# Every fifth full segment of softmax weights transposed by TensorE from fp32, and the filler spread anew

## The chip, the core and the metric

The kernel runs on one core of one Trainium2 chip. The metric is the device time of one execution in microseconds (us), as the median of the runs shown; lower is better. The profile is one execution of its own, taken by the hardware profiler.

## The reference

One decoder block in fp32 on a sequence of 4096 rows of width 1024, with 16 learned rows set before it (4112 positions). After an RMS norm one projection gives the inputs of two groups of heads: eight forgetting-attention heads (FoX) and eight RWKV-7 heads, all of width 64. Their outputs go through one output projection, the residual is added, and a final RMS norm follows.

```python
def _fox_block(q, k, v, cq, ck, q_start):          # 128 queries, all keys up to them
    s = jnp.einsum('bhqd,bhkd->bhqk', q, k).astype(jnp.float32) / math.sqrt(HEAD_DIM)
    s = s + cq[..., :, None] - ck[..., None, :]     # c: cumulated log of the forget gate
    s = jnp.where(k_pos[None, :] <= q_pos[:, None], s, NEG_INF)
    p = jax.nn.softmax(s, axis=-1)
    return jnp.einsum('bhqk,bhkd->bhqd', p, v.astype(jnp.float32))

def _rwkv7_step(S, inp):                            # a scan over 4112 positions
    r_t, w_t, k_t, v_t, a_t, b_t = inp
    sa = jnp.einsum('bhij,bhj->bhi', S, a_t)
    S = S * w_t[:, :, None, :] + sa[..., None] * b_t[:, :, None, :] + v_t[..., None] * k_t[:, :, None, :]
    return S, jnp.einsum('bhij,bhj->bhi', S, r_t)
```

## The kernel before

Precision is kept with pairs of fp16 numbers: a value is split into a high part and a remainder, and a product is made of two or three fp16 matmuls.

**Recurrence.** The rows of RWKV-7 are taken in sub-blocks of 128 positions (`subs`, 33 of them) with four chunks of 32 each; one chunk is three steps (hops) of a chain, each some small matmuls, a copy from PSUM on ScalarE and VectorE, and the next matmuls (`rwkv_chain`, matmuls psz, psu, pso). Beside each hop stand pieces of the work that prepares the sub-block after next and finishes the last one (`rwkv_pre`, `rwkv_pre2`, `rwkv_post`). `rwkv_post` ends with a normalization of the output (lines 874 to 884), TensorE transposes (psd, line 887) and a store (line 894); for the last sub-block it is called once more behind the loop, without a priority.

**Filler.** The projections of the input (`in_proj`: ps_in; queries and keys `qk_block`: ps_qk; values and gate `vz_block`: ps_vz; the other gate `gate_block`: ps_zr) are a generator, `fill`, which is drawn from in units of 48 matmuls of 256 columns: beside the recurrence each hop adds RATE = 0.33 units to a credit and draws until it is spent (line 941). What is left is drawn in attention, together with the output projection of the RWKV half (`rwkv_out`: matmuls ps_p, 24 for a tile of 128 rows, counted as 0.5 units): after each tile of attention until the share of the filler drawn, `spent`, has reached the share of the attention work done (line 1211). Where attention needs projections that aren't made yet, `projected` (line 981) draws them uncounted.

**Attention.** Heads are taken one after the other, each in 32 tiles of 128 queries. A tile's keys, 144 to 4112 of them, are cut into segments of 1024 (SEG). Score matmuls (ps_q, two PSUM buffers of 1024 columns) are evicted by VectorE (line 1051), which adds the gate's bias and keeps the running maximum; ScalarE makes the exponential in place (`sp`, fp32, line 1065) and copies it to fp16 (`hl`, line 1071); GpSimd for 60% of the segments (POOL_SHARE), else VectorE, makes the remainder (line 1076); a DMA transpose on the SP queue turns both halves at once (`ht<-hl`, 128x2048 fp16 for a full segment, line 1078); then TensorE multiplies `ht` with V (ps_o). `attention` is a generator in three parts: scores; exponential to transpose; weights times V. `advance` runs the first part of tile i, then the third of tile i-1 (`finish`), then the second of tile i. There are 9 buffers of `sp` (NSP) and 6 each of `hl` and `ht` (NHL).

**Last head.** In the eighth head the output rows of the attention half are made beside the tiles: load, TensorE transpose (ps_t, line 1233), output projection (ps_p), residual, final norm, store (`out_prep`, `out_rows`).

**Order.** The order on each engine is fixed when the program is built: a scheduler ranks instructions by their priority (an offset for attention of 100000, for filler in attention of 97000, for the chain of 300000) and by a model of when operands are ready. On the chip each engine takes its instructions in that order and waits where an operand is late. All matmuls go through `mm` (line 92); most instructions beside the recurrence are recorded under line 67.

## Time and profile before

| what | value |
|---|---|
| median of 3 runs | 4477.23 us (4459.99 to 4483.77) |
| the profiled execution | 4462.28 us, its span 4460.4 us |
| granted TensorE clock, mean over the span | 0.916 of full speed |
| TensorE (PE) busy | 3912.1 us, 88% of the span |
| VectorE (DVE) busy | 2956.9 us, 66% |
| GpSimd (POOL) busy | 2230.5 us, 50% |
| ScalarE (ACT) busy | 2122.7 us, 48% |
| DMA | 755.37 MB, mean 169 GB/s |

Busy time is the union of the instructions of an engine; matmuls overlap one another, so a burst of them counts from the first start to the last end. PEld is the weight load, beside PE. PEclk is the share of the TensorE clock that was granted, between two levels: 1.00 (2.4 GHz) and 0.50 (1.2 GHz). The DMA share is the mean busy share of the core's 16 DMA engines; packets of two queues can be under way in one engine at a time, so it can pass 1. A wait is put down to what ended it.

The kernel has stretches with different work: preparation (to about 401 us), the recurrence (to 1984), attention (first scores at 2122, last tile done at 4361), and the last output rows.

### The profile page before, as it was taken

Reading aid. Unit: us, or ns where it says so; the run is one execution under the profiler, and the core shown is the slowest. Engines: PE = TensorE matmul, PEld = TensorE weight load, DVE = VectorE, ACT = ScalarE, POOL = GpSimd, SP = SyncE. Lnnn points to the kernel's source line nnn. Section 1 sums busy time; section 2 is a strip of 40 time slices with the busy share of each in tenths; the row PEclk is TensorE's granted clock in tenths of the full one; section 3 lists DMA queues with packets and bytes.
Section 4 is the critical chain, followed back from the end, with each engine's and each line's share of the span. In section 5 each row is a group of like instructions: output and inputs, shape, how many; then the busy total and the mean of one; then the engine's idle time right before and its main releaser. Section 6 shows DMA issues by size and latency. Waiting matters only on the chain. (4 is left out here: it accounts for less than half of the span.)

```text
span 4460.4 us, 106426 instructions
## 1 busy us (share of the span) xinstructions
PE 3912.1 (88%) x42336; PEld 3012.8 (68%) x42336; DVE 2956.9 (66%) x6217; ACT 2122.7 (48%) x4338; POOL 2230.5 (50%) x3289
## 2 busy tenths in 40 slices
PE   5689999999989899998878878888888878978888
PEld 4577777777767677777656655666666656666566
DVE  5346665666667666752878978677787758646774
ACT  5433333333333233321666757577676747524552
POOL 4137565667666665762445545444454435332340
PEclk8899999999876899899999989999999989989989
DMA  9963223323222344324999999999999999999995
GB/s 265 262 172 93 79 79 97 87 75 90 74 70 79 85 138 121 98 88 141 196 213 229 216 193 227 199 216 227 208 212 234 212 203 223 258 270 242 198 218 185
DMA packets 1702644, 755.37 MB, mean 169 GB/s; under 512 B 1444601, under 2 KB 1639601, under 8 KB 1692162
## 3 DMA queue, kind: packets, MB, share of 16 engines
q1 hardware_dynamic: 1489346, 502.84, 55.8%
q10 hardware_dynamic: 194624, 170.08, 15.3%
q0 software_dynamic: 18176, 75.66, 5.6%
q8 instruction: 332, 5.44, 0.5%
q14 instruction: 166, 1.36, 0.1%
HBM read 278.97 MB, written 158.50 MB: 98 GB/s over the span
## 5 line engine op out<-in xcount | busy, mean ns | idle before, releaser
L1076 POOL TENSOR_TENSOR hl<-sp,hl 128x1024 f16<-128x1024 f32 (+7 forms) x384 | 719.7, 1881 | 517.3 <-ACT hl L1071 440.7
L1065 ACT ACTIVATE sp<-sp,nm 128x1024 f32<-128x1024 f32 (+8 forms) x672 | 644.5, 962 | 223.5 <-DVE nm L1057 175.6
L1071 ACT ACTIVATE hl<-sp 128x1024 f16<-128x1024 f32 (+8 forms) x672 | 568.2, 872 | 366.1 <-DMA ht<-hl 239.4
L92 PE MATMUL ps_o<-Vt,ht 128*128 128x64 f16 (+3 forms) x8960 | 559.5, 211 | 180.6 <-DMA ht<-hl 177.8
L92 PE MATMUL ps_q<-K,Q 128*128 128x512 f16 (+4 forms) x2432 | 596.9, 366 | 119.4 <-DVE mt L1051 118.3
L758 POOL TENSOR_TENSOR tm<-X,Am 128x248 f32<-128x248 f32 (+30 forms) x1023 | 498.1, 487 | 376.6 <-DMA Am<-a_d 290.1
L92 PEld LDWEIGHTS <-ht 128*128 128x128 f16 (+1 forms) x8960 | 466.9, 100 | 315.0 <-DMA ht<-hl 204.9
L92 PEld LDWEIGHTS <-wu 128*128 128x128 f16 (+1 forms) x5476 | 513.1, 102 | 194.8 <-ACT wu L160 28.1
L760 POOL TENSOR_TENSOR X<-X,tm 128x248 f32<-128x248 f32 (+30 forms) x1023 | 517.7, 506 | 76.6
L67 PEld LDWEIGHTS <-wu 128*128 128x128 f16 (+1 forms) x4988 | 454.5, 101 | 114.3 <-issue 26.0
L1051 DVE CUSTOM_DVE_ANT_0 sp<-ps_q,cb,mt 128x1024 f32<-128x1024 f32 (+8 forms) x416 | 436.1, 1048 | 80.3 <-PE ps_q L92 40.8
L1076 DVE TENSOR_TENSOR hl<-sp,hl 128x1024 f16<-128x1024 f32 (+8 forms) x288 | 383.2, 1333 | 99.3 <-ACT hl L1071 98.1
L92 PEld LDWEIGHTS <-Q 128*128 128x128 f16 x2432 | 221.8, 100 | 294.8 <-issue 150.2
L67 PE MATMUL ps_in<-fu,wu 128*128 128x256 f16 x3108 | 416.0, 285 | 3.4 <-DVE car L67 3.4
L1051 DVE CUSTOM_DVE_ANT_0 sp<-ps_q,cb,scs 128x1024 f32<-128x1024 f32 (+7 forms) x256 | 297.6, 1164 | 71.2 <-POOL hl L1076 43.9
L92 PE MATMUL ps_qk<-fu,wu 128*128 128x256 f16 x1632 | 237.7, 280 | 24.0 <-DVE t1k L500 18.5
L92 PE MATMUL ps_vz<-wu,fu 128*128 128x256 f16 x1644 | 247.6, 284 | 1.0 <-ACT th L544 0.6
L92 PE MATMUL ps_p<-OH,yH 128*128 128x512 f32 x512 | 221.5, 433 | 29.0 <-DVE oxt L1144 27.5
L1070 POOL MEMSET hl<- 128x224 f16 x256 | 72.4, 287 | 336.8 <-DMA ht<-hl 318.4
L92 PE MATMUL ps_zr<-fu,wu 128*128 128x256 f16 x1536 | 224.8, 285 | 8.0 <-DVE nm L1057 6.3
L67 PE MATMUL psz<-UV,SC 32*64 32x64 f32 (+1 forms) x4128 | 222.4, 232 | 3.0 <-ACT UV L67 2.2
L92 PE MATMUL ps_p<-OH,yL 128*128 128x512 f32 x512 | 209.6, 411 | 0.0
(350 smaller groups left out, 6976.6 us busy)
## 6 DMA issues: line engine op xcount, KB each, us to landing
fu<-u_d POOLq DMA_DIRECT2D x32, 1024.0 KB, 6.8
fu<-u_d SPq DMA_DIRECT2D x30, 1024.0 KB
pr<-p_d SPq DMA_DIRECT2D x32, 832.0 KB
p_d<-prt SPq DMA_DIRECT2D x96, 256.0 KB
u_d<-u SPq DMA_DIRECT2D x16, 1024.0 KB
Am<-a_d SPq DMA_DIRECT2D x128, 128.0 KB
Q<-qk_d ACTq DMA_DIRECT2D x128, 128.0 KB
oxt<-in_x_dram ACTq DMA_DIRECT2D x32, 512.0 KB
```

The costliest lines, as they stand in the source:

```text
L67: r = f(*args, **kw)
L92: PE.matmul(o, lhsT=l, rhs=r, start=start, stop=stop)
L758: G.tensor_tensor(out=tm[:, :, :k], in0=bc(X[:, :, s:s + 1], [P, 8, k]), in1=bc(Am[:, s * C + s + 1:s * C + C].unsqueeze(1), [P, 8, k]), o ...
L760: G.tensor_tensor(out=X[:, :, s + 1:], in0=X[:, :, s + 1:], in1=tm[:, :, :k], op=ALU.add)
L1051: V.tensor_tensor_reduce(out=sp[:, a - a0:b - a0], in0=ps[:, :b - a], in1=head[c][2][:, a - o:b - o], scale=scs[:, p, 0, hp:hp + 1], scala ...
L1065: A.activation(sp[:, :n], sp[:, :n], AF.Exp, bias=nm[:, 0:1], accum_out=nm[:, 1 + a // SEG:2 + a // SEG])
L1070: G.memset(hl3[:, :, n:], 0.0)
L1071: A.activation(hl3[:, 0, :n], sp[:, :n], AF.Copy)
L1076: eng.tensor_tensor(out=hl3[:, 1, :n], in0=sp[:, :n], in1=hl3[:, 0, :n], op=ALU.subtract)
```

## The change

One in five full segments (PE_SHARE = 20) of the exponentials isn't split and turned by DMA: TensorE transposes `sp` itself, in fp32, eight times 128x128, into a PSUM tile that takes its place among the score buffers (tag `q`); ScalarE copies it to fp16 as the high half of `ht`, and VectorE makes the low half from the PSUM tile and that copy. The buffers become 5 of `hl`, 8 of `sp` and 8 of `ht` (NHT); GpSimd makes the remainder of 75% of the segments that go by DMA. A tile's third part may run up to LAG = 2 tiles later, as long as the segments of the waiting tiles and the new one fit the 8 buffers of `ht`. RATE falls to 0.265. What `projected` draws is counted as `spent`, and a tile of `rwkv_out` counts 1.0. In the last head the output rows follow the tiles that are finished.

```diff
--- before.py
+++ after.py
@@ -38,15 +38,17 @@
 NREST = 26
 SEG = 1024
 CH = 1024
-NHL, NSP = 6, 9
+NHL, NSP, NHT = 5, 8, 8
+PE_SHARE = 20
 HEADS = (4, 5, 0, 1, 2, 3, 6, 7)
-POOL_SHARE = 60
+POOL_SHARE = 75
 FILL = 1.0
 PASS_OF = (2, 2, 1, 3)
 QM = 12
 PSTEP = 2
-RATE = 0.33
+RATE = 0.265
 LEAD = 6
+LAG = 2
 PARTS = ((0, 0), (0, 1), (1, 0))
 P_SHIFT = 15 * math.log(2.0)
 
@@ -980,8 +982,9 @@
 
         def projected(p, t):
 
+            nonlocal spent
             while done[PASS_OF[p]] * NB < min(t, SEQ + 1):
-                next(late)
+                spent += next(late)
 
         def head_load(h, c):
 
@@ -1008,12 +1011,13 @@
             c = min(x // CH, NCH - 1)
             return c, x - c * CH
 
-        nseg = 0
+        nseg, npe = 0, 0
+        spent = 0
         qz = {}
 
         def attention(h, i, head, dst):
 
-            nonlocal nseg
+            nonlocal nseg, npe
             p, hp = divmod(h, 2)
             q0 = 64 * hp
             if i % 4 == 0:
@@ -1064,6 +1068,18 @@
                 sp = sps[a // SEG]
                 A.activation(sp[:, :n], sp[:, :n], AF.Exp, bias=nm[:, 0:1], accum_out=nm[:, 1 + a // SEG:2 + a // SEG])
                 nt = -(-n // P)
+                ht = at.tile([P, 2 * SEG // P, P], F16, tag="ht", name="ht", bufs=NHT)[:, :2 * nt]
+                hts.append(ht)
+                if n == SEG:
+                    npe += PE_SHARE
+                    if npe >= 100:
+                        npe -= 100
+                        pt = ps_q.tile([P, nt, P], F32, tag="q", name="ps_w")
+                        for j in range(nt):
+                            PE.transpose(pt[:, j], sp[:, j * P:(j + 1) * P], ident)
+                        A.activation(ht[:, :nt], pt, AF.Copy)
+                        V.tensor_tensor(out=ht[:, nt:], in0=pt, in1=ht[:, :nt], op=ALU.subtract)
+                        continue
                 hl = at.tile([P, 2 * SEG], F16, tag="hl", name="hl", bufs=NHL)[:, :2 * nt * P]
                 hl3 = hl.rearrange("p (a k) -> p a k", a=2)
                 if n % P:
@@ -1074,9 +1090,7 @@
                     nseg += 1
                     eng = G if nseg * POOL_SHARE % 100 < POOL_SHARE else V
                 eng.tensor_tensor(out=hl3[:, 1, :n], in0=sp[:, :n], in1=hl3[:, 0, :n], op=ALU.subtract)
-                ht = at.tile([P, 2 * SEG // P, P], F16, tag="ht", name="ht", bufs=NHL)[:, :2 * nt]
                 SP.dma_start_transpose(out=ht, in_=hl)
-                hts.append(ht)
             yield
             pso = ps_o.tile([P, P], F32, tag="o", name="ps_o")
             for a, ht in zip(range(0, W, SEG), hts):
@@ -1167,39 +1181,40 @@
                 op = os_.enter_context(tc.tile_pool(name="op", bufs=2, side="left"))
                 OW = out_weights(ow, 4)
                 for _ in rwkv_out(op, OW):
-                    yield 0.5
-
-
-        left = sum(max(0, NFULL - done[i]) * n for i, n in ((1, 2), (2, 4), (3, 4))) + 0.5 * NT
+                    yield 1.0
+
+
+        left = sum(max(0, NFULL - done[i]) * n for i, n in ((1, 2), (2, 4), (3, 4))) + NT
         late = filler()
         total = left / FILL
-        work, spent = 0, 0
-        before = None
+        work = 0
+        waiting = []
+
+        segs = lambda i: -(-(N_META + P * (i + 1)) // SEG)
 
         def finish():
-            nonlocal before
-            if before is not None:
-                h, i, gen, yo = before
-                next(gen)
-                if HEADS.index(h) == 7:
-                    DQ.dma_start(yf_d[i * P:(i + 1) * P, h * HD:h * HD + HD], yo[:, i % 4])
-                elif i % 4 == 3:
-                    DQ.dma_start(yf_d[(i - 3) * P:(i + 1) * P, h * HD:(h + 1) * HD]
-                                 .rearrange("(s t) e -> t s e", t=P), yo)
-            before = None
+
+            h, i, gen, yo = waiting.pop(0)
+            next(gen)
+            if HEADS.index(h) == 7:
+                DQ.dma_start(yf_d[i * P:(i + 1) * P, h * HD:h * HD + HD], yo[:, i % 4])
+            elif i % 4 == 3:
+                DQ.dma_start(yf_d[(i - 3) * P:(i + 1) * P, h * HD:(h + 1) * HD]
+                             .rearrange("(s t) e -> t s e", t=P), yo)
 
         def advance(hx, i):
 
-            nonlocal before, yo
+            nonlocal yo
             h = HEADS[hx]
             fetch(hx, i)
             if i % 4 == 0:
                 yo = at.tile([P, 4, HD], F32, tag="yo", name="yo")
             gen = attention(h, i, heads[h], yo[:, i % 4])
             next(gen)
-            finish()
+            while waiting and (len(waiting) > LAG or sum(segs(w[1]) for w in waiting) + segs(i) > NHT):
+                finish()
             next(gen)
-            before = h, i, gen, yo
+            waiting.append((h, i, gen, yo))
 
         yo = None
         for hx in range(7):
@@ -1243,19 +1258,26 @@
             V.scalar_tensor_tensor(out=xt, in0=xt, scalar=ss[:, 1:2], in1=fnw, op0=ALU.mult, op1=ALU.mult)
             DQ.dma_start(out[i * P:(i + 1) * P], xt)
 
-        ready = None
+        ready, row = None, 0
+
+        def rows(n):
+
+            nonlocal ready, row
+            while row < n:
+                nxt = out_prep(row)
+                if ready is not None:
+                    out_rows(row - 1, *ready)
+                ready = nxt
+                row += 1
+
         for i in range(NT):
             with tc.high_priority(offset=PR[4]):
                 advance(7, i)
-            if i > 0:
-                nxt = out_prep(i - 1)
-                if ready is not None:
-                    out_rows(i - 2, *ready)
-                ready = nxt
-        finish()
-        nxt = out_prep(NT - 1)
-        out_rows(NT - 2, *ready)
-        out_rows(NT - 1, *nxt)
+            rows(waiting[0][1] if HEADS[7] == waiting[0][0] else 0)
+        while waiting:
+            finish()
+        rows(NT)
+        out_rows(NT - 1, *ready)
 
 
 _INS = ['x', 'meta', 'norm_w', 'w_in', 'b_f', 'mu_shift', 'w0', 'w_up', 'a0', 'a_up', 'k_k', 'k_a', 'r_k',
```

The line numbers of the changed kernel are 2 to 15 higher. Three places show how the order moves.

On VectorE, between the normalization of the last recurrence output and the first use of attention's loads. `Yt` (line 892, after: 894) finishes that output, `identb` (line 975, after: 977) is the first write into the buffers of attention, `cb` the bias of the first head; `qk`, `vt` and `t1k` are evictions of filler. Before:

```order
L67 SCALAR_TENSOR_TENSOR t1k<-t1k 128x256
L67 TENSOR_TENSOR t1k<-t1k,fnb 128x256
L67 SCALAR_TENSOR_TENSOR qk<-ps_qk,sqs,qk 128x256
L67 SCALAR_TENSOR_TENSOR qk<-ps_qk,qk 128x256
L494 SCALAR_TENSOR_TENSOR vt<-ps_vz,vt 128x2x64 x2
L500 TENSOR_TENSOR t1k<-ps_vz,fnb 128x256
L892 TENSOR_TENSOR Yt<-Yt,bon 128x128
L975 CAST identb<-ident 128x128
L503 SCALAR_TENSOR_TENSOR t1k<-t1k 128x256
L505 TENSOR_TENSOR t1k<-t1k,fnb 128x256
L998 TENSOR_SCALAR cb<-cb,scs 128x1024 x3
```

After, from the normalization's last step (line 886) on:

```order
L886 TENSOR_TENSOR Y<-Y,gva 32x512
L505 SCALAR_TENSOR_TENSOR t1k<-t1k 128x256
L183 TENSOR_SCALAR ss<-pss 128x1
L507 TENSOR_TENSOR t1k<-t1k,fnb 128x256
L894 TENSOR_TENSOR Yt<-Yt,bon 128x128
L977 CAST identb<-ident 128x128
L195 SCALAR_TENSOR_TENSOR wst<-wst,psb 128x1024
L199 COPY fnb<-psb 128x128
L462 TENSOR_SCALAR fnb<-fnb 128x128
L1001 TENSOR_SCALAR cb<-cb,scs 128x1024 x3
```

Before, 52 rows of filler's evictions stand between that step (line 884) and the row of `Yt`; now there are 3. On TensorE 912 filler matmuls stand before the transposes of this output, and now 48.

On VectorE in attention, the scores of tile 30 (counted from 0, four segments) of the fourth head (line 1051, after: 1055, is the eviction of scores; `mt` its maximum; `nm` the maximum or the sums of a tile). Before:

```order
L1051 ISA sp,mt<-ps_q,cb,scs 128x1024
L1051 ISA mt 128x1
L545 SCALAR_TENSOR_TENSOR zt_40139<-th_40140,zt_40139 128x512
L1076 TENSOR_TENSOR hl<-sp,hl 128x1024
L1051 ISA sp,mt<-ps_q,cb,mt,scs 128x1024
L1051 ISA mt 128x1
L1051 ISA sp,mt<-ps_q,cb,mt,scs 128x1024
L1051 ISA mt 128x1
L1096 TENSOR_REDUCE nm<-nm 128x1
L1100 TENSOR_TENSOR o_41699<-ps_o,o_41699 128x64
L1097 RECIPROCAL nm<-nm 128x1
```

After, from the tile's second segment on; line 1081 makes the low half from the TensorE transposes in PSUM:

```order
L1055 ISA sp,mt<-ps_q,cb,mt,scs 128x1024
L1055 ISA mt 128x1
L1081 TENSOR_TENSOR ht<-ps_w,ht 128x1024
L1114 TENSOR_TENSOR o_42277<-ps_o,o_42277 128x64
L1115 SCALAR_TENSOR_TENSOR yo<-o_42277,nm,Zt 128x64
L1055 ISA sp,mt<-ps_q,cb,mt,scs 128x1024
L1055 ISA mt 128x1
L1055 ISA sp,mt<-ps_q,cb,mt,scs 128x912
L1055 ISA mt 128x1
L1061 TENSOR_SCALAR nm<-mt 128x1
```

Before, a filler eviction, a remainder (line 1076, SBUF to SBUF) and the end of an earlier tile stood between the score evictions. Now the row of line 1081, for a segment of an earlier tile, stands there; the score matmul that takes its PSUM buffer is issued behind it.

On the SP queue, tiles of the first head with one, two and three segments (the middle number is twice the segment's columns over 128). Before:

```order
L1078 DMA_TRANSPOSE ht<-hl 128x12x128
L1078 DMA_TRANSPOSE ht<-hl 128x16x128
L1078 DMA_TRANSPOSE ht<-hl 128x14x128
L1078 DMA_TRANSPOSE ht<-hl 128x16x128 x4
L1078 DMA_TRANSPOSE ht<-hl 128x2x128
L1078 DMA_TRANSPOSE ht<-hl 128x16x128 x2
L1078 DMA_TRANSPOSE ht<-hl 128x4x128
L1078 DMA_TRANSPOSE ht<-hl 128x16x128 x2
```

After:

```order
L1093 DMA_TRANSPOSE ht<-hl 128x12x128
L1093 DMA_TRANSPOSE ht<-hl 128x16x128
L1093 DMA_TRANSPOSE ht<-hl 128x14x128
L1093 DMA_TRANSPOSE ht<-hl 128x16x128 x3
L1093 DMA_TRANSPOSE ht<-hl 128x2x128
L1093 DMA_TRANSPOSE ht<-hl 128x16x128 x2
L1093 DMA_TRANSPOSE ht<-hl 128x4x128
L1093 DMA_TRANSPOSE ht<-hl 128x16x128
L1093 DMA_TRANSPOSE ht<-hl 128x6x128
L1093 DMA_TRANSPOSE ht<-hl 128x16x128 x2
```

The rows stand in the same sequence; where a full segment goes to TensorE its row is missing.

## Rows read from the trace of the kernel before

**Rows 1.** Five stretches: time, busy time (instructions) by engine, PEclk, DMA share, GB/s.
```profile
core 0: us, PE busy (x) PEld busy (x) DVE busy (x) ACT busy (x) POOL busy (x), PEclk, DMA share, GB/s
401.00:1984.00 1583.00, 1524.57 (x19786) 1197.15 (x19784) 1022.50 (x2242) 520.02 (x1302) 1033.12 (x2025) 0.91 0.32 89
1984.00:2085.00 101.00, 100.69 (x924) 90.07 (x923) 28.98 (x80) 18.25 (x47) 31.23 (x45) 1.00 0.30 109
2085.00:2122.00 37.00, 18.50 (x153) 15.58 (x151) 6.99 (x15) 1.55 (x4) 6.21 (x15) 0.72 0.83 223
2122.00:4361.00 2239.00, 1884.84 (x18027) 1397.21 (x18025) 1649.51 (x3403) 1391.23 (x2660) 996.61 (x907) 0.93 1.12 220
4361.00:4460.00 99.00, 86.43 (x392) 68.20 (x390) 49.75 (x74) 24.62 (x44) 8.11 (x15) 0.97 0.50 184
```

**Rows 2.** TensorE's timeline: start, length (us), instructions that follow one another.
```profile
1982.55 0.66 PE L67 MATMUL psd<-ident,Y 128*128 128x128 f32 x4
1983.28 5.41 PE L67 MATMUL ps_vz<-wu,fu 128*128 128x256 f16 x48
1988.53 1.69 PE L67 MATMUL ps_qk<-fu,wu 128*128 128x256 f16 x14
```

**Rows 3.** VectorE's timeline behind the recurrence.
```profile
1994.18 0.68 DVE L884 TENSOR_TENSOR Y<-Y,gva 32x512 f32<-32x512 f32 x1 [1.56 <-POOL gva L882]
2084.63 0.29 DVE L892 TENSOR_TENSOR Yt<-Yt,bon 128x128 f32<-128x128 f32 x1 [0.26 <-ACT Yt L891]
2098.56 0.76 DVE L998 TENSOR_SCALAR cb<-cb,scs 128x1024 f32<-128x1024 f32 x1 [12.71 <-DMA cb<-c_d]
```

**Rows 4.** TensorE's waits in attention: us in all, times, longest.
```profile
PE ps_o L92 <- DMA ht<-hl: 177.8, 87, 11.0
PE ps_q L92 <- DVE mt L1051: 118.3, 104, 7.1
```

**Rows 5.** SP queue: timeline of attention; its issues (ns min/median/max).
```profile
2125.56 2224.22 SPq L1078 DMA_TRANSPOSE ht<-hl  x672
...
L1078 SPq DMA_TRANSPOSE ht<-hl x672: 1167/2134/12831, 2125.6 to 4347.2; - x168
```

**Rows 6.** DMA queues of the page: packets, MB, share of 16 engines.
```profile
q1 hardware_dynamic: 1489346, 502.84, 55.8%
q0 software_dynamic: 18176, 75.66, 5.6%
```

**Rows 7.** The four quarters (8 tiles each) of the second head.
```profile
2384.00:2413.00 29.00, 25.28 (x251) 18.42 (x249) 23.25 (x64) 21.29 (x50) 12.84 (x18) 0.96 1.03 221
2413.00:2458.00 45.00, 40.94 (x445) 30.04 (x442) 43.91 (x95) 34.79 (x69) 24.05 (x22) 1.00 1.10 215
2458.00:2520.00 62.00, 54.53 (x582) 41.33 (x581) 54.92 (x103) 45.53 (x84) 34.45 (x28) 0.94 1.11 220
2520.00:2636.00 116.00, 86.58 (x928) 63.21 (x927) 85.26 (x167) 65.02 (x120) 54.65 (x54) 0.87 1.22 209
```

**Rows 8.** Groups by shape: xcount, busy us, mean ns, idle before, releasers.
```profile
L1071 ACT ACTIVATE hl<-sp 128x1024 f16<-128x1024 f32 x416 | 430.0, 1050 | 193.9 <-DMA ht<-hl 126.1 <-issue 17.5 <-PE ps_q L92 9.8
L1076 POOL TENSOR_TENSOR hl<-sp,hl 128x1024 f16<-128x1024 f32 x240 | 532.6, 2223 | 412.3 <-ACT hl L1071 338.6 <-issue 29.8 <-DMA fnw<-in_final_norm_w_dram 19.6
L1076 DVE TENSOR_TENSOR hl<-sp,hl 128x1024 f16<-128x1024 f32 x176 | 271.5, 1543 | 53.3 <-ACT hl L1071 52.4 <-DMA Zt<-zf_d 0.6
L1051 DVE CUSTOM_DVE_ANT_0 sp<-ps_q,cb,scs 128x1024 f32<-128x1024 f32 x200 | 255.3, 1276 | 56.9 <-POOL hl L1076 33.3 <-PE ps_q L92 20.8 <-PE ps_o L92 0.7
```

**Rows 9.** The output rows' TensorE transposes, line 1233: ns min/median/max.
```profile
L1233 PEld LDWEIGHTS ps_t<-ident,yf x128: 137/140/231, 4090.1 to 4440.6; 128*128 128x128 f32 x128
L1233 PE MATMUL ps_t<-ident,yf x128: 269/273/476, 4090.1 to 4440.7; 128*128 128x128 f32 x128
```

**Rows 10.** Two sub-blocks of the recurrence: one without filler, one with.
```profile
1382.00:1435.00 53.00, 50.63 (x529) 38.67 (x527) 40.45 (x89) 14.27 (x37) 31.77 (x63) 0.50 0.30 81
1645.00:1695.00 50.00, 50.00 (x666) 39.55 (x664) 32.37 (x69) 16.68 (x43) 32.35 (x67) 1.00 0.43 118
```

## The prediction

> **What bounds the kernel now.** I read the profile first as five stretches: the recurrence, a gap behind it, the wait for the first attention loads, attention, and the tail after the last attention tile [rows 1]. In the recurrence TensorE is busy 1524.6 of 1583 us, so it idles 58 us or 3.7%: this stretch is as long as TensorE's work, chain and filler together. The 101 us behind it (1984 to 2085) hold nothing but filler: 924 matmuls, busy 100.7 us, one every 0.109 us (48 matmuls from 1983.28 to 1988.53) [rows 1, 2]. VectorE's timeline shows why that hurts: the last step of the recurrence's output (line 884) is done at 1994.2, the step behind it (line 892) comes at 2084.6, because its TensorE transpose stands behind the filler; the first attention loads, which take over its buffers, are used only at 2098.6 [rows 3]. So here filler holds up attention.
>
> In attention (2122 to 4361) TensorE is busy 1884.8 of 2239 us: 354 us idle, 15.8% [rows 1]. Half of this is one wait: the weights-times-V matmuls wait for the DMA transposes, 177.8 us in 87 waits; the score matmuls wait for a free score buffer, which VectorE empties, 118.3 us [rows 4]. The DMA engines stand behind the first: their share is 1.12 over the stretch [rows 1], the SP queue issues its 672 transposes from 2125.6 on over 2224 us, one per 3.3 us, while single issues took from 1.2 to 12.8 us, 2.1 in the median [rows 5]. In the quarters of one head the idle share of TensorE is 13%, 9%, 12% and 25%, and the DMA share is highest, 1.22, in the last [rows 7]. So attention is bound by TensorE and the transposes together, the last quarter of each head by the transposes.
>
> **The change part by part**, against the profiled execution: 4462.3 us, of which 4460.4 are its span. The median of the runs shown, 4477.2, is 15 us higher, and I add that at the end.
>
> Less filler beside the recurrence. By the built order 6096 filler matmuls stand between the chain's first and last matmul now, 5760 after: 336 fewer at 0.109 us is 37 us. Between the chain's last matmul and the first score matmul stand 1074 now and 201 after: 873 fewer, 95 us. The wait for the first loads, 37 us, stays. What this uncovers: the chain's own latency, which is covered by 58 us of idle time only, so I take both terms whole and keep 0 for the first as the other end (see the rivals).
>
> Attention gets the filler: 1209 matmuls more, 132 us of TensorE time.
>
> The TensorE transposes: one in five full segments is 83 segments, 664 transposes of 128x128 in fp32. Four such transposes of the recurrence take 0.66 us from the start of the first to the end of the last, with 0.27 us for one alone, so one follows the other in 0.13 us [rows 2, 9]; the weight load of one takes 0.14 us [rows 9]. At 0.14 us this is 93 us; with each standing alone at 0.273 us it would be 181 us, which I keep for the range, and nothing here lets them cost less than 0.13, 86 us. I take 93, as they are issued by eights.
> By the Trainium skill (TensorE: Matmul & The Clock Gate, Part 4: PE-mode transpose) a 128x128 bf16 transpose costs some 275 ns in a kernel. By that the 664 would be an estimated 183 us, 90 us more, and the forecast some 4500 us. The rows' 0.14 us decides, since they are fp32 transposes of this kernel, issued one behind the other.
>
> The DMA transposes that go: 83 of 128x2048 fp16, 0.524 MB each, 43.5 MB. The SP queue's packets took 55.8% of the 16 engines' span for 502.8 MB, 4.95 us per MB [rows 6], so 215 us of engine time go. The moved filler, 25 units of 48 matmuls, brings about 13.5 MB (a 1 MB block of activations for four units, and their outputs) on GpSimd's queue at 3.3 us per MB [rows 6]: 45 us. DMA time in attention goes from 1.12 x 2239 = 2508 to 2338 us: a share of 1.00 over the length forecast below.
>
> The other engines. ScalarE makes 83 copies from PSUM instead of 83 from SBUF, 1.05 us each [rows 8]: nothing, since it is busy 1391 of 2239 us. VectorE's subtractions go from 288 to 172 and 83 from PSUM, between the 1.28 us of a score eviction, which reads PSUM too, and 1.54 us [rows 8]: some 50 us less on an engine that is 74% busy, so no gain counted. GpSimd's go from 384 to 417, 33 x 2.22 = 73 us on an engine busy 997 of 2239 us: hidden; if its cover is gone, 33 x 0.68 = 22 us for the slower engine. One buffer fewer for the fp16 pairs and for the scores stands against a fifth fewer users: counted at nothing.
>
> The tail. After the last weights-times-V matmul stand 336 output matmuls now and 144 after. The tail's 392 matmuls take 86.4 us [rows 1], 0.22 us each; 192 of them, 42 us, move into attention.
>
> The idle time is the large unknown. TensorE's work in attention becomes 1885 + 132 + 93 + 42 = 2152 us. Its idle share now is 15.8%; the recurrence, dense with filler and with a DMA share of 0.32, has 3.7%. These are my ends. I take 8%, near the 9% that a second quarter of a head has now [rows 7]: the DMA share falls, two more buffers for transposed weights and the longer lag give a transpose a tile more of time, and there is 24% more filler to stand between the waits (4950 matmuls now, 6159 after). Attention is then 2152 / 0.92 = 2339 us, 100 us longer.
> Sum: -37 - 95 + 100 - 42 = -74 us; 4388, and on the scale of the medians 4403 us.
> From it follows the point of decision: the medians' 4477 is met at 261 us of idle time in attention (10.8%), and each us of idle time is a us of the result.
>
> **The rivals.**
> 1. The score buffers take over from the DMA wait. The transposes write to the two PSUM buffers of the scores. One of the 83 holds its buffer for the ScalarE copy and the VectorE subtraction, 1.05 + 1.54 us, and by the new order the next score stands behind it on VectorE. For: score matmuls wait 118 us already, and ScalarE and VectorE work in order. Against: VectorE is 74% busy, filler can stand in between. If 1 us of each 2.6 is filled, 83 x 1.6 = 133 us come in while the wait for transposes falls to a third, -118: idle time 369 us, and the time is 4403 + 182 = 4585 us. It decides from 261 us of idle time on.
> 2. The recurrence doesn't get shorter. A sub-block without filler had a granted clock of 0.50 and took 53 us, one full of filler at 1.00 took 50 us [rows 10]: what the filler gives back, the clock takes. Against: four fifths of the filler stays. Then the 37 us are lost: 4440 us; the 95 us of the gap, where no chain runs, stay.
> 3. The transposes pull the clock down in attention. It is at 0.93 over the stretch [rows 1] and at 0.87 in the last quarter of a head [rows 7]; of the two levels, 1.2 and 2.4 GHz, the lower then holds for 14% and for 26% of the time. If all of attention fell to 0.87, 12% of 2339 us more would run at half speed: 281 us, of which 92% busy, and half of that is lost, 129 us: 4532 us. Against it: of the 128 transposes of the output rows the median is 273 ns and the longest 476 [rows 9], so most ran at the higher level.
> The same Part 4 of the Trainium skill says that transposes don't count as TensorE activity for the clock; what rows show of it is that median alone, and here they stand between other matmuls.
> 4. The new order keeps everything busy as in the recurrence, 3.7% idle: 2235 us of attention, 4299 us.
>
> **How the numbers follow.** Forecast 0.50, rival 1 0.24, rival 2 0.12, rival 3 0.08, rival 4 0.06. Range: it leaves out the far end of rival 1 and the end of rival 4: 4320 (4.6% idle) to 4550 us (13.4% idle); the forecast's own range, 6% to 10.5% idle, is 4353 to 4469. About 0.5%, 22 us, is what a measurement of this kernel can tell from no change, so faster needs under 239 us idle, slower over 283. Faster: most of the forecast (0.41), most of rival 2 (0.09), rival 4 (0.06): 0.56. Slower: rival 1 and rival 3 mostly, and a little of the forecast: 0.28. The rest, 0.16, is no change.
>
> **What would show it.** Between the recurrence's last step and the first score about 95 us fewer; the recurrence some 37 us shorter, at a clock of 0.90 or more. In attention 664 transposes about 0.14 us apart, a DMA share near 1.0, the wait for transposes under 90 us and that for score buffers not over 150. A tail near 57 us. The forecast is wrong if attention takes over 2413 us: then either the score buffers' wait has grown (rival 1), the clock is lower (rival 3), or the wait for DMA stayed near 178 us although the share fell.

## The result and the profile after

The changed kernel takes 4630.07 us (median of 4 runs, 4621.53 to 4669.09) against 4478.23 us before (4 runs, 4459.99 to 4483.77): 1.036 times as long, 95% interval 1.030 to 1.043. The forecast was 4403 us, faster; its range ended at 4550. The profiled execution of the changed kernel is its longest, 4669.1 us, so the two profiles differ by 207 us where the medians differ by 152.

The stretches after, which answer to [rows 1] (time, busy time of each engine, granted clock, DMA share); the pure filler behind the recurrence is gone as a stretch of its own:

```profile
core 0: us, PE busy (x) PEld busy (x) DVE busy (x) ACT busy (x) POOL busy (x), PEclk, DMA share, GB/s
401.00:1967.00 1566.00, 1482.25 (x19490) 1162.56 (x19487) 1022.06 (x2226) 519.33 (x1292) 1019.83 (x2009) 0.91 0.31 88
1967.00:2002.00 35.00, 21.86 (x155) 17.42 (x155) 9.88 (x20) 3.46 (x9) 7.35 (x15) 0.75 0.81 213
2002.00:4621.00 2619.00, 2178.02 (x20127) 1655.85 (x20125) 1719.63 (x3500) 1423.50 (x2735) 1091.82 (x1006) 0.91 0.87 181
4621.00:4667.00 46.00, 36.54 (x170) 29.06 (x167) 22.02 (x33) 10.73 (x20) 3.85 (x7) 0.96 0.46 167
```

Attention begins 120 us earlier (2002 for 2122) and the tail is 53 us shorter, but attention itself takes 2619 us for 2239. TensorE works 293 us more in it, and idles 2619 - 2178 = 441 us, 16.8%, where the forecast had 8%. The DMA engines, which the forecast saw behind that idle time, are less loaded than it hoped: a share of 0.87, some 2280 us of their time for the 2338 forecast. Yet the wait for them grew. TensorE's waits after, against [rows 4], and two waits that name the cause, on VectorE and ScalarE:

```profile
PE ps_o L94 <- DMA ht<-hl: 266.6, 115, 12.3
PE ps_q L94 <- DVE mt L1055: 53.0, 43, 10.8
PE ps_w L1079 <- ACT sp L1069: 24.6, 14, 4.4
DVE sp L1055 <- PE ps_q L94: 326.4, 237, 10.8
ACT sp L1069 <- DVE nm L1061: 383.2, 128, 12.4
```

The same two waits in the kernel before (us in all, times, longest), and the largest wait of the SP queue's transposes for their input, before and after:

```profile
DVE sp L1051 <- PE ps_q L92: 64.7, 55, 4.3
ACT sp L1065 <- DVE nm L1057: 175.6, 91, 14.5
SPq L1078 <- POOL hl L1076: 256.8, 135, 7.4
SPq L1093 <- POOL hl L1092: 731.5, 172, 15.6
```

Read them as a chain. VectorE now waits 326 us for score matmuls, 65 before: the scores come late, and no longer for want of a free buffer (53 us for 118). ScalarE then waits 383 us for the maximum that closes a tile's scores, 176 before. So the exponential, the fp16 pair and the transpose all start late, and the weights-times-V matmuls wait for the transpose although its queue has room: the queue itself waits 732 us for GpSimd's remainders, 257 before. GpSimd makes a larger share of them now, but in e3, below, with its share of before, the queue waits 440 us for GpSimd's and 468 for VectorE's (96 before).

Why the scores are late is in the timeline of TensorE at the end of the fourth head (start, length, instructions in a row, in brackets the idle time ahead of them):

```profile
3217.64 1.03 PE L94 MATMUL ps_q<-K,Q 128*128 128x512 f16 x4
...
3219.70 0.17 PE L94 MATMUL ps_q<-dmask,identb 128*128 128x16 bf16 x1
...
3225.72 3.72 PE L94 MATMUL ps_vz<-wu,fu 128*128 128x256 f16 x21 [3.65 <-ACT th L546]
3236.12 3.04 PE L94 MATMUL ps_o<-Vt,ht 128*128 128x128 f16 x32 [6.68 <-DMA ht<-hl]
3238.97 0.46 PE L1079 MATMUL ps_w<-ident,sp 128*128 128x128 f32 x1
3239.22 0.45 PE L94 MATMUL ps_q<-K,Q 128*128 128x144 f16 x2
```

of VectorE, the eviction of tile 31's last scores:

```profile
3228.88 0.28 DVE L1055 CUSTOM_DVE_ANT_0 sp<-ps_q,cb,mt 128x16 f32<-128x16 f32 x1
```

and of ScalarE, the first and the last exponential of the same tile:

```profile
3229.58 1.15 ACT L1069 ACTIVATE sp<-sp,nm 128x1024 f32<-128x1024 f32 x1 [3.91 <-DVE nm L1061]
...
3234.12 0.29 ACT L1069 ACTIVATE sp<-sp,nm 128x16 f32<-128x16 f32 x1
```

The last scores of tile 31 are done at 3219.9. The next scores (144 keys, tile 0 of the next head) start at 3239.2, behind the first TensorE transpose of tile 31's exponentials. The pool hands out its two buffers in the order in which the program asks for them, and the program asks for the transposes' buffer between the scores of one tile and those of the next. So the next scores can't be issued before this tile's exponential is there, 19 us in which TensorE has filler, idles 3.65 and 6.68 us, and has no score to do. Not all of the 19 us is the exponential, which ends at 3234.4: VectorE evicts the last scores only 9 us after they are done, behind other work, and the 32 products that stand ahead of the transposes on TensorE (tile 30's) wait for their own DMA until 3236.1. The built order shows the same loss of distance: behind the last score of tile 29 of the fourth head stands the weights-times-V product of tile 26 in the kernel before, and that of tile 28 in the changed one. The scores ran three tiles ahead of the products, and now run one. Counted so in the traces, over tiles 20 to 31 of all heads, the scores' lead is 3.2 tiles on average before and 1.3 after.

The steps that came as forecast: VectorE behind the recurrence, against [rows 3]:

```profile
1965.74 0.67 DVE L886 TENSOR_TENSOR Y<-Y,gva 32x512 f32<-32x512 f32 x1
1968.49 0.29 DVE L894 TENSOR_TENSOR Yt<-Yt,bon 128x128 f32<-128x128 f32 x1 [1.08 <-ACT Yt L893]
1980.51 0.75 DVE L1001 TENSOR_SCALAR cb<-cb,scs 128x1024 f32<-128x1024 f32 x1 [1.97 <-DMA cb<-c_d]
```

Here 2.8 us lie between the two steps that were 90 us apart. And the transposes themselves (ns min/median/max), beside [rows 8, 9]:

```profile
L1079 PEld LDWEIGHTS ps_w<-ident,sp x664: 137/141/231, 2044.7 to 4595.9; 128*128 128x128 f32 x166
L1079 PE MATMUL ps_w<-ident,sp x664: 270/273/476, 2044.8 to 4596.0; 128*128 128x128 f32 x166
L1080 ACT ACTIVATE ht<-ps_w x83: 1000/1024/1042, 2047.9 to 4605.7; 128x1024 f16<-128x1024 f32 x83
L1081 DVE TENSOR_TENSOR ht<-ps_w,ht x83: 1206/1219/1226, 2049.0 to 4606.8; 128x1024 f16<-128x1024 f32 x83
```

664 of them, each counted to the start of the next matmul or to its own end, make 89 us, 0.134 us each. One alone lasts 273 ns, near the some 275 ns that the Trainium skill (TensorE: Matmul & The Clock Gate, Part 4: PE-mode transpose) gives for a bf16 one in a kernel; but that is the length of one, and in a row they follow at half of it, so here that figure is no price for a batch.

### The profile page after: what moved, and what is told of

Read it like the earlier page. It is cut to its first block, busy times and chain, and to the rows that moved or that the text cites. A ratio compares the mean times of both kernels' runs of the same rounds, so it can differ in the third digit from the quotient of the medians.

```text
span 4667.3 us, 107386 instructions
## 1 busy us (share of the span) xinstructions
PE 4021.0 (86%) x43000; PEld 3112.4 (67%) x43000; DVE 2970.4 (64%) x6184; ACT 2124.5 (46%) x4338; POOL 2279.9 (49%) x3322
## 5 line engine op out<-in xcount | busy, mean ns | idle before, releaser
L1092 POOL TENSOR_TENSOR hl<-sp,hl 128x1024 f16<-128x1024 f32 (+7 forms) x417 | 778.9, 1882 | 539.8 <-ACT hl L1087 513.3
L94 PEld LDWEIGHTS <-ht 128*128 128x128 f16 (+1 forms) x8960 | 476.3, 102 | 406.8 <-DMA ht<-hl 301.9
L94 PE MATMUL ps_q<-K,Q 128*128 128x512 f16 (+4 forms) x2432 | 609.0, 372 | 62.3 <-DVE mt L1055 53.0
L1055 DVE CUSTOM_DVE_ANT_0 sp<-ps_q,cb,mt 128x1024 f32<-128x1024 f32 (+8 forms) x416 | 437.2, 1051 | 192.6 <-PE ps_q L94 163.5
L1087 ACT ACTIVATE hl<-sp 128x1024 f16<-128x1024 f32 (+8 forms) x589 | 475.8, 843 | 112.8 <-DMA ht<-hl 66.5
L94 PE MATMUL ps_vz<-wu,fu 128*128 128x256 f16 x2280 | 319.4, 282 | 8.5 <-ACT th L546 4.5
L94 PE MATMUL ps_qk<-fu,wu 128*128 128x256 f16 x2208 | 307.7, 280 | 20.4 <-DVE t1k L502 16.0
L1092 DVE TENSOR_TENSOR hl<-sp,hl 128x1024 f16<-128x1024 f32 (+8 forms) x172 | 254.4, 1481 | 30.5 <-ACT hl L1087 28.7
L94 PEld LDWEIGHTS <-fu 128*128 128x128 f16 x2472 | 231.0, 101 | 54.8 <-issue 11.4
```

The lines of the kernel that those rows point to most:

```text
L94: PE.matmul(o, lhsT=l, rhs=r, start=start, stop=stop)
L1055: V.tensor_tensor_reduce(out=sp[:, a - a0:b - a0], in0=ps[:, :b - a], in1=head[c][2][:, a - o:b - o], scale=scs[:, p, 0, hp:hp + 1], scala ...
L1087: A.activation(hl3[:, 0, :n], sp[:, :n], AF.Copy)
L1092: eng.tensor_tensor(out=hl3[:, 1, :n], in0=sp[:, :n], in1=hl3[:, 0, :n], op=ALU.subtract)
```

## The experiments

Three theories stood at the start: A, the turn among the score buffers; B, the rest of the change (filler, lag, buffers, GpSimd's share); C, the transposes' own TensorE time and clock. For the filler came later D, a burst of filler drawn at once, and E, the lower rate itself. Times in the second column are medians; the kernel before was timed again beside each group of runs (medians 4476 to 4484 us), and ratios and differences to before are to that time. The other columns are of the profiled execution; "idle" is TensorE's in attention, the waits are those of [rows 4].

| run | us | ratio to before (95%) | attention us | idle | wait for DMA | wait for score buffer |
|---|---|---|---|---|---|---|
| before | 4478 | | 2239 | 354 | 178 | 118 |
| the change | 4630 | 1.036 (1.030 to 1.043) | 2619 | 441 | 267 | 53 |
| e1 change, no TensorE transposes | 4525 | 1.011 (1.003 to 1.019) | 2386 | 367 | 183 | 133 |
| e2 change, turn of their own | 4476 | 1.000 (0.997 to 1.004) | 2344 | 289 | 57 | 108 |
| e3 before + transposes | 4679 | 1.044 (1.037 to 1.051) | 2527 | 461 | 265 | 83 |
| e4 before + filler part | 4538 | 1.012 (1.004 to 1.020) | 2372 | 376 | 170 | 126 |
| e5 before + the turn only | 4697 | 1.051 (1.045 to 1.056) | 2520 | 501 | 324 | 55 |
| e6 change, half hold | 4809 | 1.075 (1.071 to 1.079) | 2764 | 528 | 308 | 61 |
| e7 before + transposes, own turn | 4431 | 0.990 (0.986 to 0.994) | 2214 | 280 | 78 | 87 |
| e8 e2 with before's filler numbers | 4463 | 0.999 (0.995 to 1.003) | 2190 | 298 | 24 | 167 |
| e9 before, gap closed | 4428 | 0.989 (0.985 to 0.993) | 2255 | 336 | 139 | 120 |
| e10 before, lower rate | 4529 | 1.011 (1.007 to 1.016) | 2366 | 383 | 195 | 115 |
| e11 e7, GpSimd 75% | 4479 | 1.000 (0.997 to 1.003) | 2253 | 305 | 48 | 131 |
| e12 e7, three in ten | 4503 | 1.007 (1.003 to 1.011) | 2319 | 304 | 24 | 135 |
| e13 before + burst | 4495 | 1.002 (0.999 to 1.005) | 2225 | 377 | 177 | 145 |
| e14 e10, no burst | 4499 | 1.004 (1.001 to 1.007) | 2347 | 367 | 145 | 155 |
| e15 e7 + e9 | 4425 | 0.986 (0.982 to 0.990) | 2288 | 293 | 77 | 132 |
| e16 e2, no burst | 4477 | 1.000 (0.996 to 1.004) | 2354 | 309 | 54 | 154 |

**Which part of the change is it?** e1:

```diff
-PE_SHARE = 20
+PE_SHARE = 0
```

> The changed kernel with no segment transposed by TensorE (all 672 go by DMA); everything else of the change stays (filler order, the lag, 5 and 8 and 8 buffers, GpSimd's 75%). Theory A (the TensorE transposes take their turn among the score buffers, so the next tile's scores stand behind the exponential of this tile, and a DMA transpose gets less TensorE work to hide behind): weights-times-V waits for DMA fall from 267 us to 180 or less, attention loses 150 to 250 us, the time is 4380 to 4500 us. Theory B (the transposes aren't it: the filler now in attention, the lag, the buffers or GpSimd's larger share are): the wait stays over 230 us, only the 93 us of TensorE's transposing go, 4530 us or more. Theory C (the transposes cost their own TensorE time and the clock, not the order): 4630 less 90 to 140, 4490 to 4540, with the DMA wait unchanged.

4525 us: 105 us come back, the wait falls to 183 us and attention loses 233 us. That is C's time with what A said of attention and, nearly, of the wait, so e1 alone doesn't decide. The change without its transposes is still 41 us slower than before, so the rest of it costs too. e4 took that rest apart: the kernel before with RATE 0.265, `projected` counted, the weight 1.0 and the output rows behind the finished tiles.

> The kernel before with the filler part of the change alone (the lower rate beside the recurrence, the draws counted, the weight 1.0, the output rows after the finished tiles) and no TensorE transposes, lag, buffers or GpSimd share. Theory A and theory C: attention gets 1209 filler matmuls, has 262 us less DMA-bound idle time to lose than the forecast took, and ends between 4400 and 4490 us. Theory B: the filler costs attention more than the recurrence and the gap give back, 4540 us or more.

4538 us, 54 us slower, nearest to B: the filler, forecast as a gain, is a loss (below). And e3, before plus the branch of the changed `attention` that transposes on TensorE (line 1073 to 1082), with before's 6 and 9 buffers:

> The kernel before with one full segment in five transposed by TensorE as in the changed kernel, among the score buffers, and nothing else of the change. Theory A: slower than before by 100 to 200 us, 4580 to 4680 us, with a DMA wait of over 230 us. Theory B: within 40 us of before plus the transposes' own time where it isn't hidden, 4440 to 4530 us. Theory C: 4540 to 4590 us, with the DMA wait at 178 us or less.

4679 us, 195 us slower, with the DMA wait at 265 us as A said, though by the forecast only 93 us of work came in.

**The turn, taken away.** e2:

```diff
-                        pt = ps_q.tile([P, nt, P], F32, tag="q", name="ps_w")
-                        for j in range(nt):
...
+                        for j0 in range(0, nt, 4):
+                            pt = ps_o.tile([P, 4, P], F32, tag="o", name="ps_w")
...
-            pso = ps_o.tile([P, P], F32, tag="o", name="ps_o")
+            pso = ps_o.tile([P, 4, P], F32, tag="o", name="ps_o")[:, 0]
```

> The changed kernel with the TensorE transposes in PSUM buffers that they share with the weights-times-V products (four transposes to a buffer) and no longer with the scores. Theory A: the scores run ahead again, the wait for DMA falls under 180 us, TensorE idles 190 to 300 us in attention, the time is 4400 to 4510 us, though all 664 transposes stay. Theory B: no change, 4600 us or more. Theory C: no change, 4600 us or more.

4476 us, 154 us less than the change, with all 664 transposes still there. Its waits:

```profile
PE ps_q L94 <- DVE mt L1055: 107.7, 103, 6.2
PE ps_o L94 <- DMA ht<-hl: 56.5, 21, 11.1
DVE sp L1055 <- PE ps_q L94: 65.8, 66, 4.0
```

and its attention as a stretch, with the columns of [rows 1]:

```profile
2013.00:4357.00 2344.00, 2054.52 (x19847) 1573.73 (x19845) 1644.28 (x3533) 1410.19 (x2788) 1069.67 (x996) 0.94 0.97 197
```

VectorE's wait for scores is back at 66 us and the wait for DMA is a fifth of the change's; TensorE idles 289 us. In the built order the product behind the last score of tile 29 is that of tile 25, and the lead over tiles 20 to 31 is 3.25 tiles. The granted clock of attention is 0.94 with the transposes, 0.93 before [rows 1], so they don't pull it down here.

**The turn, alone.** e2 also halved the size of a transposed piece. Two runs separate the turn from that and from the work. e5, in the kernel before, with PE_SHARE = 20:

```diff
...
+                if n == SEG:
+                    npe += PE_SHARE
+                    if npe >= 100:
+                        npe -= 100
+                        pt = ps_q.tile([P, P], F32, tag="q", name="ps_w")
+                        PE.transpose(pt, sp[:, :P], ident)
+                        A.activation(nm[:, 6:7], pt[:, 0:1], AF.Copy)
```

> The kernel before, all segments by DMA; for one full segment in five a single 128x128 TensorE transpose of the exponentials goes into a score buffer, and ScalarE reads one column of it, which nothing uses. That is the turn among the score buffers without the work: 83 transposes, 12 us of TensorE. Theory A (the turn pins the next scores behind the exponential): the wait of weights-times-V for DMA rises over 220 us, the time is 4540 to 4640 us. Theory C, and the view that it is the time for which a transposed segment holds its buffer (1.05 and 1.54 us for the copy and the subtraction): within 25 us of before, 4510 us at most.

4697 us, 215 us slower, more than A's 4640, by 83 transposes that nothing uses. They and the column that ScalarE reads (ns min/median/max):

```profile
L1073 PE MATMUL ps_w<-ident,sp x83: 270/308/477, 2183.2 to 4631.3; 128*128 128x128 f32 x83
L1074 ACT ACTIVATE nm<-ps_w x83: 143/153/194, 2183.6 to 4633.7; 128x1 f32<-128x1 f32 x83
```

and its waits:

```profile
PE ps_o L93 <- DMA ht<-hl: 324.1, 143, 14.2
DVE sp L1052 <- PE ps_q L93: 301.8, 179, 10.9
```

and its attention as a stretch:

```profile
2133.00:4653.00 2520.00, 2019.20 (x18359) 1478.79 (x18357) 1678.67 (x3446) 1416.14 (x2770) 1019.79 (x916) 0.89 0.99 200
```

The DMA share is 0.99, nearly that of e2 (0.97), with a wait of 324 us where e2 has 57; the scores' lead is 1.8 tiles.

A buffer held for 0.15 us by ScalarE in place of 1.02 + 1.22 us costs the same and more: neither the hold nor the work decides, but the place in the turn. e6, the changed kernel with e2's loop of four transposes but in the score buffers (`ps_q`, tag `q`):

> The changed kernel with the TensorE transposes among the score buffers as they are, but four to a buffer in place of eight: the same form as in the run with the turn of their own, and each holds its buffer half as long. Theory A: 4600 to 4680 us, the wait for DMA over 240 us. The view that the hold decides: half of the loss comes back, 4480 to 4570 us.

4809 us. With half the hold and twice the turns it is slower still, above A's own range, with a lead of 1.0. It differs from e2 by 333 us, and in its edit by the pool alone (e2 also gives a product's buffer the size of four transposes).

**The transposes on their own turn in the kernel before.** e7 is e3 with e2's edit; e8 is e2 with RATE 0.33, weight 0.5, `projected` not counted.

> The kernel before with one full segment in five transposed by TensorE in the buffers of the weights-times-V products; filler, lag, buffers and GpSimd's share as before. The filler part alone cost 54 us, and the changed kernel with the turn of its own is level with before, so by theory A this is 4410 to 4460 us, with a DMA wait under 90 us. If the two don't add up (the filler that the change brings to attention is what fills its idle time), 4470 to 4530 us.

> The changed kernel with the turn of its own and the filler numbers of before (rate 0.33, weight 0.5, draws by attention's loads not counted); lag, 5 and 8 and 8 buffers, GpSimd's 75% and the output rows as in the change. By theory A 4400 to 4450 us; against the run with before's lag and buffers it shows what these are worth: I expect within 25 us of it, since the waits they ease (weights-times-V for DMA) are small once the scores run ahead. If the filler is needed in attention, 4470 to 4530 us.

e7: 4431 us, 1.0% faster than before, as forecast from the parts, with a lead of 3.6 (e3, among the score buffers: 1.1). e8: 4463 us, outside its 4400 to 4450 and 31 us slower than e7: lag, buffers, GpSimd's 75% and the output rows together bring no gain but a loss. Two variations of e7 missed:

> The kernel before with the TensorE transposes in the buffers of the weights-times-V products, and GpSimd's share of the remainders at 75%. The largest wait of attention is then that of the scores for VectorE's evictions (87 us); VectorE loses some 60 subtractions. If that wait follows: 4395 to 4425 us. If GpSimd's slower subtraction delays the transposes, the wait for DMA grows over 78 us: 4440 to 4480 us.

> The kernel before with the TensorE transposes in the buffers of the weights-times-V products, for three full segments in ten in place of two. 42 segments more cost some 42 us of TensorE time; the wait for DMA, 78 us, has at most that to give. I expect 4420 to 4470 us, no gain over one in five; under 4410 us would show that the DMA engines' load still decides.

e11, 4479 us, has the time of its second case but not its reason: the wait for DMA fell (48 us), and that for VectorE's evictions rose to 131 us in place of falling. GpSimd's share of 75% alone is 48 us slower than e7 and takes all that e7 gains. e12, 4503 us: 24 us of DMA wait, 135 us for evictions, and 2319 us of attention. Why the eviction wait grows in both isn't shown.

**The filler.** e9 sets a priority:

```diff
-        for _ in rwkv_post(sts.pop(len(subs) - 1)):
-            pass
+        with tc.high_priority(offset=PR[1]):
+            for _ in rwkv_post(sts.pop(len(subs) - 1)):
+                pass
```

> The kernel before, with the last output steps of the recurrence given the priority that the recurrence's other steps have, so that they no longer stand behind the filler: by the built order 413 matmuls stand between the chain's last one and the first score, 1083 before; 670 filler matmuls (73 us) go from there into attention and the tail. If the filler then fills idle time of attention, as the forecast took it: 4400 to 4440 us. If filler is worth the same wherever it stands, since TensorE was 100% busy in that stretch and the idle time of attention comes from waits that filler doesn't end: 4465 to 4520 us.

> The kernel before with the rate of filler beside the recurrence at 0.265 in place of 0.33, nothing else: 336 filler matmuls (37 us) leave the recurrence, and by the built order 869 fewer stand behind the chain. If the 54 us of the filler part came from the recurrence idling in place of the filler (27 us more idle time there in that run) and from attention's own idle time: 4500 to 4550 us. If they came from the counted draws and the weight 1.0, which this run lacks: 4470 to 4495 us.

e9 is 51 us faster: the gap did hold attention up, as forecast. e10, the rate alone, is 49 us slower although it closes the gap too. e9 by stretch (up to the chain's end, to the first score, attention, tail):

```profile
401.00:2007.00 1606.00, 1539.77 (x19983) 1210.19 (x19982) 1042.17 (x2272) 525.51 (x1313) 1047.71 (x2042) 0.91 0.32 89
2007.00:2048.00 41.00, 33.84 (x289) 29.12 (x288) 10.56 (x26) 5.57 (x16) 10.77 (x21) 0.92 0.81 240
2048.00:4303.00 2255.00, 1919.43 (x18617) 1439.25 (x18616) 1680.74 (x3438) 1396.42 (x2678) 1016.86 (x935) 0.94 1.10 220
4303.00:4423.00 120.00, 104.37 (x471) 82.54 (x470) 60.54 (x89) 29.64 (x53) 9.76 (x18) 0.98 0.51 183
```

Against [rows 1], 591 matmuls fewer ahead of attention save 74 us, 590 more in it cost 16 us, and the tail is 21 us longer. What was left open was whether the lower rate loses by a burst: its schedule leaves projections undone that the next heads' loads need, so 65 units of filler (44 in the change, none before) are drawn at once in the third head.

> The kernel before; ahead of tile 17 (counted from 0) of the third head 44 units of filler are drawn at once and at attention's priority, and counted; the total is the same. The changed kernel draws so many there, because the loads of the next heads need projections that the lower rate has left undone (65 with the rate alone, none before). Theory D (the burst is what the filler part costs): the third head takes 330 us or more, and the time is 4510 to 4540 us. Theory E (a recurrence with less filler idles more, 27 us, and attention has no idle time to give; the burst only moves filler): 4470 to 4500 us.

> The kernel before at the rate 0.265, with filler drawn 1.35 times as fast in the first three heads of attention and slower behind them, so that no unit is drawn because a load needs it. Theory D: the 49 us of the rate go and the closed gap counts: 4430 to 4480 us. Theory E: as with the rate alone, 4510 to 4540 us.

e13 decides nothing: 4495 us isn't told from before, and the third head took 252 us, so the scheduler had spread the 44 units. e14, whose draws are `while spent < total * min(1.35 * w, 1 - 0.737 * (1 - w))` with w the share of tiles done, takes 4499 us, between D and E: 30 of the 49 us are back. It has e9's closed gap and is 71 us slower than e9:

```profile
401.00:1980.00 1579.00, 1493.35 (x19512) 1169.41 (x19508) 1024.30 (x2229) 518.86 (x1293) 1017.37 (x2012) 0.91 0.32 88
1980.00:2017.00 37.00, 23.42 (x166) 18.62 (x166) 10.15 (x21) 3.93 (x10) 7.64 (x17) 0.73 0.75 203
2017.00:4364.00 2347.00, 1980.49 (x19094) 1492.90 (x19093) 1686.40 (x3468) 1396.23 (x2694) 1035.18 (x959) 0.93 1.06 213
4364.00:4496.00 132.00, 116.80 (x528) 92.68 (x528) 67.10 (x98) 33.03 (x59) 10.95 (x20) 0.98 0.52 188
```

594 matmuls fewer ahead of attention save 31 us, 0.05 us each; 477 more in it cost 92 us, 0.19 us each, where one takes 0.109 us [rows 1]. Beside the recurrence half of the removed filler comes back as idle time and slower matmuls (idle up to the chain's end 66 us in e9, 86 in e14); in attention the first 590 were nearly free, the next 477 are not. By head, e14 against e9 loses in the third (321 us for 260) and in the eighth (399 for 341), and the other six together are faster. In the third the scores' lead is 1.7 tiles, 3.0 in e9, though no unit is drawn for a load; why it is short there isn't shown.

**The whole.**

> The kernel before with the two parts that were faster alone: the TensorE transposes in the buffers of the weights-times-V products (50 us), and the priority for the last output steps of the recurrence (51 us). If they add up, 4370 to 4400 us; if both took the same idle time of attention, 4410 to 4440 us.

> The changed kernel with the turn of its own for the TensorE transposes and the faster draws in the first three heads, so without the burst. If the turn and the burst are all that kept the forecast from coming true: 4400 to 4440 us, near the 4403 forecast. If the lower rate itself costs (theory E): 4465 to 4490 us, as with the turn alone.

e16, 4477 us, is level with e2, in E's range: with the turn mended, the burst is worth nothing. That the lower rate keeps the change from its forecast, as E said, isn't shown by it: e8 has the rate of before and is only 14 us faster than e2, not told from before either (0.995 to 1.003), and the larger loss against e7 is the 31 us of lag, buffers, GpSimd's share and output rows. Nor did e16 spread the filler evenly: its sixth head still takes 379 us, 254 in e8. e15 is the fastest, 4425 us, 1.4% faster than before (0.982 to 0.990) and 4.4% under the changed kernel. Its parts don't add up: it lies within 6 us of e7 and of e9, since the 626 matmuls that the gap gives to attention cost 74 us there (2214 to 2288 us), not 16, and ahead of it save 96.

## Why the prediction was wrong

- **The step that failed is the idle time of attention**: "I take 8%". It was 16.8%, 441 us for 187; these 254 us are nearly all of the 281 us between the forecast's sum (-74) and the difference of the profiles (+207); 26 more are TensorE's work in attention (2178 us for 2152). The step took idle time as set above all by the DMA engines' load, and the load did fall (0.87); of the prediction's own signs of being wrong it is the last that came, a wait for DMA that stays although the share falls. But a tile's products wait for the latency of its own chain, scores to transpose, and what covers that is how far the scores run ahead. The turn cut this; e2 undoes it, e5 makes it without the work.
- **Rival 1 had the place and not the mechanism.** It priced the hold of a score buffer, 83 x 1.6 us, and expected the wait for buffers to rise and that for DMA to fall to a third. The reverse came: 118 to 53, 178 to 267. The turn has no term in it. Its 4585 us is nearer by chance.
- **Less filler beside the recurrence**: the 132 us for loop and gap measured 120 us in the start of attention, so the term held in sum: the gap gave more than its 95 us (138 us between the recurrence and the first score before, 35 after), the loop 17 of its 37. There TensorE is busy 42 us less and idles 25 us more (58 to 84) at an unchanged granted clock of 0.91, so idle time took the rest, and not rival 2's clock. Wrong was to add the filler to attention at its own 0.109 us: e14 against e9 shows 0.19. The gap was a real gain (e9, 51 us net); the lower rate in the loop was a loss.
- **Right**: the transposes (93 us forecast, 89; in e2, counted so, 79, which is under the 86 that the prediction took for the least), the gap, the tail (42, measured 53), and the low chance of rival 3: the granted clock fell to 0.91, not to 0.87, and not by the transposes, since e2 with 664 of them has 0.94 and e5 with 83 has 0.89.
- **A term put at nothing**: GpSimd's larger share was taken as hidden (22 us if its cover is gone). In e11 it costs 48 us against e7, in a kernel with the filler of before; how much of that is in the change itself isn't shown.
- **The sign** hung on more than the turn: e2 shows that even without it the change is level with before. Two forecast gains, the filler's and the lag's, didn't come (e4, e8).
- The signs were there to read: in [rows 4] the scores wait 118 us for VectorE, which itself waited only 65 us for scores (64.7 above), so the scores ran ahead; and the change lets an instruction that needs this tile's exponential ask for a buffer ahead of the next tile's scores.

Open: the 20 to 70 us that the lower rate still costs in e14 (against before and against e9), the eviction wait in e11 and e12, and the spread of some tens of us between schedules that differ little.

## What to carry to other kernels

Buffers of one tag are given out in program order, so a late-stage user put among the buffers of an early stage makes the next early stage wait for the late one; ask of each new user of a shared buffer what it waits for, not only how long it holds. In a pipeline bound by a latency, look at how far the first stage runs ahead before and after (here in the built order and in VectorE's wait for scores), ahead of any engine's load. Moving filler is worth the idle time that it ends; here the second piece gave back less than the first and cost more.

## What the runs showed of the hardware

The DMA share of attention fell from 1.12 to 0.87 while the wait for DMA rose from 178 to 267 us, and e2 and e5, with shares of 0.97 and 0.99, waited 57 and 324 us: the load alone didn't tell the wait. 128x128 fp32 transposes issued by eights took 0.134 us each though one lasts 273 ns, and 664 of them left the granted clock of e2's attention at 0.94. The Trainium skill (Perfetto Trace Analysis, Optimization Strategy) says that gaps that repeat can mean too few buffers for the next tile; the runs agree only in part, since in e5 the same two score buffers, with 83 turns of 0.15 us more, brought 147 us more idle time (354 to 501).
